# Gate-row buffers of the Fourier group moved into the room of the projection weights, and the loads of the last two stages put in another order on one queue

## The chip, the core and the metric

One core of a Trainium2 chip runs one program. The metric is the device time of one execution in microseconds (us), the median of several runs. The core's engines are TensorE (PE, with its weight load PEld), VectorE (DVE), ScalarE (ACT) and GpSimd (POOL); SyncE (SP) issues every transfer of this kernel, in the order in which they stand in its program, so all transfers share one queue.

## What is computed

One layer of a mixer over 2048 latent tokens of width 1024, with a prefix of 256 context tokens. One projection of the normalised input feeds two groups of heads, and their outputs go through one output projection:

```python
hx = rmsnorm(x, norm_w) * (1 + scale) + shift
u, zf, zs, xbc, dt = split(hx @ w_in)          # 512, 512, 1536, 2560, 48 columns
mixed = fft2(u, axes=(positions, 64 channels)).real @ w_fourier + b_fourier
four  = mixed * silu(zf)                       # Fourier group: 512 columns
xbc = silu(conv3x3(xbc) + conv_b)              # depthwise, then a scan over chunks of 128
y   = scan_forward(xbc, dt) + scan_backward(xbc, dt) + d_skip * xs
ssd = rmsnorm_by_group(y * silu(zs)) * ssd_norm_w
out = rmsnorm(x + gate * (concat(four, ssd) @ w_out)) * final_norm_w
```

## The kernel before, in words

All of it is fp32. A matrix product is done as three fp32r products of high and low parts (`hh`, `hl` hold the two parts of the normalised input for all tokens, 64 KB of each partition apiece; `wh`, `wl` those of one 128-column tile of projection weights). What each engine does next is fixed when the program is built: a scheduler lays out the instructions that the code issues, within their dependencies, and each engine then works through its own list in order.

The end of the kernel has three stages that matter here.

**Backward scan.** It runs beside projections of the gate columns `zs`, for token blocks 0 to 2. A weight tile is loaded by `weights` (L164 to L171) into `raw` (one buffer), split by ACT into `wh` and by POOL into `wl` (two buffers each), and used by 24 matmuls for each token block (L176 to L178). These buffers are in pool `wp` (stack `p1w`).

**Fourier stage** (from L863). Twelve weight tiles are loaded again for token block 3, `zs_ops([(i, (3,)) ...])`. `interleave` puts the Fourier work between their matmuls: `f_table` (from the loaded `w_fourier` and the 64-point tables), `f_step2` (the second step of the transform, from `g_d` and `tw`), and `f_mm(dt, h, i)`: 16 calls of 12 matmuls for four column tiles `dt` and two halves `h`. `f_gate` follows each pair: it adds the bias, and multiplies with the gate rows `zf` of that `dt`, a tile of 128 x 2048 (1 MB) that `zf_load` brings from `zfT_d`; pool `fb` has two such buffers. After its second half, `fm_d<-zf` stores the gated tile. What `interleave` has not placed is returned as `left` and issued afterwards.

**Unit stage** (`s1` to `s6`): 64 units (16 chunks by 4 groups). `s1` builds the decay matrix of a unit (small loads `rt`, `lt`, then `cb`, `chl`), `s2` and `s3` carry the state, `s4` and `s5` form and normalise the output, and `s6` multiplies with the output weights. These weights (16 MB as high and low parts) are loaded by `w_group(0)` to `w_group(3)`, eight loads of 512 KB each, into the rooms of `hh` and `hl` as these come free: group 0 after the last projection, group 1 after the `h = 0` half of the last `f_mm`, groups 2 and 3 after the `h = 1` half. `s6` of unit u needs group u mod 4, and for the Fourier columns a piece of `fm_d` (`fm_half`): columns 0 and 1 for groups 0 and 1, columns 2 and 3 for groups 2 and 3. `tc.issue_after(x)` keeps what is issued under it behind x on its queue.

As built, each transfer on SP's queue also waits until the transfer eight places ahead of it has landed, so at most eight are under way.

Of the kernel before, what the change touches and what calls it, by code (L numbers as in the profile page):

```python
# [9 lines left out]
F32 = mybir.dt.float32  # L10
# [8 lines left out]
P = 128  # L19
# [30 lines left out]
def mixer_layer(ctx: ExitStack, tc: tile.TileContext, A: dict, out: bass.AP, taps=None):  # L50
# [3 lines left out]
    def pool(name, bufs=1, space=None, stack=ctx, side=None):  # L54
        kw = {"space": space} if space is not None else {}
        if side is not None:
            kw["side"] = side
        if space != DRAM:
            kw["reuse_waits"] = "tile"
        return stack.enter_context(tc.tile_pool(name=name, bufs=bufs, **kw))  # L60
# [6 lines left out]
    def copy(dst, src):  # L67
        return nc.scalar.activation(dst, src, AF.Copy).ins  # L68
# [29 lines left out]
    def const_tile(name, where=const):  # L98
        a = A[name]
        t = where.tile(list(a.shape), F32, name="c_" + name)  # L100
        load(t, a)
        return t
# [37 lines left out]
    p1 = ctx.enter_context(ExitStack())  # L140
# [5 lines left out]
    p1w = ctx.enter_context(ExitStack())  # L146
# [609 lines left out]
    def interleave(main, side, lead, speed, finish=False):  # L756
        tm, ts = (sum(c for c, _ in o) for o in (main, side))
        am = as_ = 0.0
        n = 0
        for c, fn in main:  # L760
            fn()
            am += c
            while n < len(side) and am >= lead and as_ <= speed * ts * (am - lead) / tm:
                side[n][1]()
                as_ += side[n][0]
                n += 1
        for _, fn in side[n:] if finish else ():
            fn()
        return side[n:]

    with ExitStack() as psc:
        sp = pool("sp3", 2, stack=psc)
        st = {}
# [85 lines left out]
    def w_group(g):  # L859
        for n in range(4 * g, 4 * g + 4):  # L860
            w_load(n)

    pfb = ctx.enter_context(ExitStack())  # L863
    pfa = ctx.enter_context(ExitStack())
    fa = pool("fa", 2, stack=pfa)
    fb = pool("fb", 2, stack=pfb, side="right")
    c64 = [const_tile("c64", where=fa), const_tile("s64", where=fa)]
    tw64 = const_tile("tw64", where=fa)
    bf = const_tile("bf", where=fb)
    xe = fb.tile([P, 2, 2, 4, 16], F32R, name="xe", bufs=1)  # L870
    ye = fb.tile([P, 4, 16], F32, name="ye", bufs=1)
    fo = {"new": main_psum}
    gls = {}
    tws = {}
    zft = {}
# [19 lines left out]

    def zf_load(dt):
        def go():
            zf = zft[dt] = fb.tile([P, 16, P], F32, name="zf", tag="zf")
            load(zf[:].rearrange("p a b -> p (a b)"), zfT_d[dt])
            if dt != 2:  # L900
                nc.scalar.activation(zf, zf, AF.Silu)
            nc.gpsimd.tensor_tensor(out=zf[:, :, 64], in0=zf[:, :, 64], in1=ye[:, dt], op=ALU.mult)
        return go
# [41 lines left out]
    def f_gate(dt, p0, p1, parts):  # L945
        zf = zft[dt]
        q32 = fb.tile([P, 512], F32, name="q32", tag="q32", bufs=1)
        copy(q32, p1)
        for sign in range(2):
            yy = fb.tile([P, 512], F32, name="yy", tag="yy")  # L950
            nc.vector.scalar_tensor_tensor(out=yy, in0=p0, scalar=bf[:, dt:dt + 1], in1=q32,
                                           op0=ALU.add, op1=ALU.add if sign == 0 else ALU.subtract)
            for yv, k1, nt in parts[sign](yy):
                a = k1 if sign == 0 else P - k1 - nt * yv.shape[-1] + 1
                zv = zf[:, :, a:a + nt * yv.shape[-1]]
                if sign == 1:
                    zv = rev(zv)
                if nt > 1:
                    zv = zv.rearrange("p a (t b) -> p t a b", t=nt)
                (nc.vector if sign else nc.gpsimd).tensor_tensor(out=zv, in0=yv, in1=zv, op=ALU.mult)  # L960
# [44 lines left out]
    tw_load(0)  # L1005
    g_load(0, 0)
    P2 = {}
    dts = [0, 3, 1, 2]
    side = [(1.7, f_table(j)) for j in range(4)]
    for b in range(4):  # L1010
        side += [(0.9, f_step2(b, ct)) for ct in range(4)]
# [2 lines left out]
        if b == 1:  # L1014
            side += [(0.0, zf_load(dt)) for dt in dts[:2]]
    side.append((0.0, f_switch))
    fmm = [(dt, h) for dt in dts[:2] for h in range(2)] + [(dt, h) for h in range(2) for dt in dts[2:]]
    for n, (dt, h) in enumerate(fmm):
        if n in (4, 5):
            side.append((0.0, zf_load(dt)))  # L1020
        if n == 6:
            side.append((0.0, lambda: w_group(1)))
        side += [(2.6, f_mm(dt, h, i)) for i in range(2)]
    left = interleave(zs_ops([(i, (3,)) for i in range(19, 7, -1)]), side, 10, .75)
    wa1 = P2["wa1"]
    ones = const_tile("ones", wa1)
    msk = wa1.tile([P, P], U8, name="msk8", bufs=1)
# [11 lines left out]
    for t in lt:  # L1039
        nc.vector.tensor_copy(out=t, in_=st2[:, :2])  # L1040

    w_group(0)
    for _, fn in left:
        fn()
    p1.close()
    ps = pool("ps2", space=PSUM)
    fo["new"] = lambda: ps.tile([P, 512], F32, name="pft", tag="out", bufs=2)
# [39 lines left out]
    for u in range(2):  # L1087
        s1(u)
    pfb.close()
    p1w.close()  # L1090
    wk = pool("wk", 2)
    fnw = const_tile("fnw", wk)
    wa = pool("wa", 2)
# [151 lines left out]

    NU = NCH * G
    s2(0)
    for u in range(NU + 2):
        if u + 1 < NU:
            if u > 0:  # L1250
                s1(u + 1)
            s2(u + 1)
        if u < 2:
            with tc.issue_after(fo["st"]), tc.issue_after(units[u + 1]["ld"]):
                w_group(u + 2)
        if u < NU:
            s3(u)
            s4(u)
        if 1 <= u <= NU:
            s5(u - 1)  # L1260
        if u >= 2:
            s6(u - 2)
# [110 lines left out]
```

## Time and profile before

| | |
|---|---|
| time, median of 3 runs | 1911.37 us (1909.71 to 1916.48) |
| the profiled execution: its own time | 1912.61 us |
| its span, first to last instruction | 1910.8 us |
| PE busy | 1809.4 us, 95% of the span |
| DVE, ACT, POOL busy | 1258.5, 873.9, 906.2 us |
| mean granted TensorE clock | 0.977 |
| moved by SP's queue | 300 MB, 50.6% of the DMA engines' time |

The median of the runs stands 1.2 us below the profiled execution, and 1.8 us of that execution lie around its span. Busy times of PE are modelled ends of pipelined matmuls, so what PE waits for, and when it starts again, says more than its busy share.

### The profile page before, as it was taken

To read this page: it belongs to the slowest core of one execution; us is meant where nothing else is said; L and a number is where in the kernel's file an instruction comes from. 1 tells how busy PE (TensorE), PEld (TensorE's weight loads), DVE (VectorE), ACT (ScalarE), POOL (GpSimd) and SP (SyncE) were. 2 spreads that over 40 slices of the span, in tenths; PEclk is the share of its full clock that TensorE was granted. 3 is DMA by queue.
4 is the path that set the end of the run, shared out by engine and by line. 5 is a ranking of instruction groups with operands and counts; after the bars stand their busy time and mean duration, and the time that the engine had idled before them with its cause. 6 is when DMAs were issued, how large, how long until landed. Compare 5 with 4: busy or idle time off the path is not lost.

```text
span 1910.8 us, 28132 instructions
## 1 busy us (share of the span) xinstructions
PE 1809.4 (95%) x9142; PEld 1492.4 (78%) x9142; DVE 1258.5 (66%) x1809; ACT 873.9 (46%) x1968; POOL 906.2 (47%) x791
## 2 busy tenths in 40 slices
PE   6989999999999999989999999957999999999997
PEld 2779988888888888878888877845778777777776
DVE  3744569788888897557665622334677777667865
ACT  3632235445445455346666653223444444435443
POOL 1320034224123134178787732145777777668742
PEclk8999999999999999999999999977999999999999
DMA  7432344535445345367776774786445444444441
GB/s 256 166 93 77 90 131 151 171 113 166 138 130 160 122 129 174 120 200 217 213 218 206 216 247 136 224 287 218 125 143 151 130 132 134 147 124 138 144 137 44
DMA packets 291332, 301.80 MB, mean 158 GB/s; under 512 B 34098, under 2 KB 242066, under 8 KB 290675
## 3 DMA queue, kind: packets, MB, share of 16 engines
q1 hardware_dynamic: 291186, 300.01, 50.6%
q8 instruction: 73, 1.20, 0.3%
q14 instruction: 73, 0.59, 0.1%
HBM read 196.82 MB, written 103.10 MB: 157 GB/s over the span
## 4 chain that ended last, share of the span: by engine, by line
PE 75%; DMA 9%; DVE 5%; POOL 5%; issue 3%; ACT 2%; SPq 1%; POOLq 0%; DVEq 0%; ACTq 0%
PE pj L178 11%; PE pj L177 11%; PE pj L176 11%; PE po L1212 6%; PE po L1210 6%; PE po L1211 6%; PE py L1151 2%; PE parg L1079 2%; POOL sl L72 2%; PE pj L508 1%; PE pj L509 1%; PE pj L510 1%; PE py L1154 1%; DMA ev<-in_wout 1%; PE ptr L569 1%
## 5 line engine op out<-in xcount | busy, mean ns | idle before, releaser
L178 PE MATMUL pj<-hh,wl 128*128 128x512 f32 x1152 | 452.6, 393 | 0.8 <-POOL wl L72 0.8
L177 PE MATMUL pj<-hl,wh 128*128 128x512 f32 x1152 | 452.1, 392 | 0.0
L176 PE MATMUL pj<-hh,wh 128*128 128x512 f32 x1152 | 450.0, 394 | 2.1 <-ACT img L68 1.6
L636 DVE SCALAR_TENSOR_TENSOR pacc<-img,c_convw,pacc 128x1024 f32<-128x1024 f32 x320 | 410.0, 1287 | 58.5 <-ACT pacc L633 49.2
L72 POOL TENSOR_TENSOR wl<-raw,wh 128x1024 fp32r<-128x1024 f32 x48 | 116.5, 2428 | 345.4 <-ACT wh L68 294.8
L178 PEld LDWEIGHTS pj<-hh,wl 128*128 128x128 f32 x1152 | 216.4, 188 | 47.4 <-POOL wl L72 1.4
L176 PEld LDWEIGHTS pj<-hh,wh 128*128 128x128 f32 x1152 | 217.0, 188 | 44.4 <-ACT img L68 2.3
L177 PEld LDWEIGHTS pj<-hl,wh 128*128 128x128 f32 x1152 | 216.6, 188 | 40.9 <-issue 1.8
L807 ACT ACTIVATE xd<-xt,smb 128x64 f32<-128x64 f32 x384 | 100.8, 336 | 80.2 <-POOL yb L811 78.5
L1210 PE MATMUL po<-hl,mh 128*128 128x512 f32 x288 | 117.5, 408 | 0.7 <-ACT mh L68 0.4
L1211 PE MATMUL po<-hh,mh 128*128 128x512 f32 x288 | 114.8, 399 | 0.0
L1081 DVE COPY_PREDICATED parg<-msk,parg 128x384 f32<-128x384 uint8 x128 | 71.1, 556 | 64.1 <-PE parg L1079 63.7
L1212 PE MATMUL po<-hl,ml 128*128 128x512 f32 x288 | 109.8, 401 | 2.6 <-POOL ml L72 2.4
L1083 ACT ACTIVATE w<-parg 128x384 f32<-128x384 f32 x128 | 62.3, 486 | 104.8 <-DVE parg L1081 104.5
L72 DVE TENSOR_TENSOR xl<-xw,xh 128x384 fp32r<-128x384 f32 x76 | 63.7, 843 | 59.3 <-ACT xh L68 57.9
L1120 POOL TENSOR_TENSOR ts<-ts,yb 128x384 f32<-128x384 f32 x64 | 73.6, 1150 | 57.6 <-issue 27.2
L1079 PE MATMUL parg<-rt,lt 128*128 128x384 f32 x256 | 88.0, 372 | 11.2 <-DMA rt<-cum_d 4.1
L72 POOL TENSOR_TENSOR ml<-gt,mh 128x384 fp32r<-128x384 f32 x64 | 68.4, 1068 | 58.8 <-ACT mh L68 55.4
L68 ACT ACTIVATE xh<-xw 128x384 fp32r<-128x384 f32 x136 | 69.9, 516 | 55.2 <-PE pst L1138 14.9
L1084 DVE TENSOR_TENSOR w<-w,cb 128x768 f32<-128x768 f32 x64 | 81.6, 1275 | 12.1 <-ACT w L1083 10.9
L72 DVE TENSOR_TENSOR sl<-hbk,sh 128x384 fp32r<-128x384 f32 x64 | 59.9, 937 | 38.4 <-ACT sh L68 38.2
L72 POOL TENSOR_TENSOR sl<-ev,sh 128x512 fp32r<-128x512 f32 x32 | 42.1, 1317 | 89.1 <-DMA wo_d<-sl 38.3
(388 smaller groups left out, 4132.7 us busy)
## 6 DMA issues: line engine op xcount, KB each, us to landing
raw<-in_win SPq DMA_DIRECT2D x48, 512.0 KB
xt<-xtok_d SPq DMA_DIRECT2D x80, 192.0 KB
xtok_d<-tk SPq DMA_DIRECT2D x48, 256.0 KB
zsT_d<-ev SPq DMA_DIRECT2D x48, 256.0 KB
yb_d<-yb SPq DMA_DIRECT2D x64, 192.0 KB
yb<-yb_d SPq DMA_DIRECT2D x64, 192.0 KB
zs<-zsT_d SPq DMA_DIRECT2D x64, 192.0 KB
xg<-xtok_d SPq DMA_DIRECT2D x64, 192.0 KB
```

The costliest lines, as they stand in the source:

```text
L72: (lo_engine or nc.vector).tensor_tensor(out=lo, in0=src, in1=hi.bitcast(F32), op=ALU.subtract)
L176: mm(po, wh[:, k], a, start=(k == 0), stop=False)
L177: mm(po, wh[:, k], b, start=False, stop=False)
L178: done["mm"] = mm(po, wl[:, k], a, start=False, stop=(k == KT - 1)).ins
L636: nc.vector.scalar_tensor_tensor(out=acc, in0=im[:, r0 + dy:r0 + dy + 16, dx:dx + GRID_W], scalar=tap(t), in1=acc, op0=ALU.mult, op1=ALU.add)
L807: nc.scalar.activation(xd[:, h], d["x"][:, h], AF.Copy, scale=smb[:, 3, c, g * HG + h:g * HG + h + 1])
L1079: mm(po, l[:, dr], r[:, cols], start=True, stop=True)
L1084: nc.vector.tensor_tensor(out=w, in0=w, in1=cb[:].unsqueeze(1).broadcast_to([P, HG, P]), op=ALU.mult)
L1120: nc.gpsimd.tensor_tensor(out=ts, in0=ts, in1=yb, op=ALU.add)
L1210: mm(po, a, wh[:, i], start=(g == 0 and q == 0), stop=False)
L1211: mm(po, a, wl[:, i], start=False, stop=False)
L1212: mm(po, b, wh[:, i], start=False, stop=(g == 3 and q == 3))
```

## The change

The pool of projection weights `wp` is closed at the start of the Fourier stage, and a new one of the same kind, `wp2`, opened behind the pool `fb`. `wp2` in turn is closed after the last projection, and a pool `fz` with two buffers for gate rows takes its room. The order of the column tiles becomes 0, 1, 3, 2. All work of the first two is interleaved with the projections; the other two, with their gate rows loaded into `fz`, follow. Weight group 1 is issued between their halves, as before; group 2 is issued right after `s2(0)`, group 3 after `s2(1)`, and neither is kept behind the last store of gated rows.

```diff
--- before.py
+++ after.py
@@ -863,13 +863,17 @@
     pfb = ctx.enter_context(ExitStack())
     pfa = ctx.enter_context(ExitStack())
     fa = pool("fa", 2, stack=pfa)
+    p1w.close()
     fb = pool("fb", 2, stack=pfb, side="right")
+    p2w = ctx.enter_context(ExitStack())
+    W["p"] = pool("wp2", 2, stack=p2w, side="right")
     c64 = [const_tile("c64", where=fa), const_tile("s64", where=fa)]
     tw64 = const_tile("tw64", where=fa)
     bf = const_tile("bf", where=fb)
     xe = fb.tile([P, 2, 2, 4, 16], F32R, name="xe", bufs=1)
     ye = fb.tile([P, 4, 16], F32, name="ye", bufs=1)
     fo = {"new": main_psum}
+    fz = {"p": fb}
     gls = {}
     tws = {}
     zft = {}
@@ -895,7 +899,7 @@
 
     def zf_load(dt):
         def go():
-            zf = zft[dt] = fb.tile([P, 16, P], F32, name="zf", tag="zf")
+            zf = zft[dt] = fz["p"].tile([P, 16, P], F32, name="zf", tag="zf")
             load(zf[:].rearrange("p a b -> p (a b)"), zfT_d[dt])
             if dt != 2:
                 nc.scalar.activation(zf, zf, AF.Silu)
@@ -945,7 +949,7 @@
     def f_gate(dt, p0, p1, parts):
         zf = zft[dt]
         q32 = fb.tile([P, 512], F32, name="q32", tag="q32", bufs=1)
-        copy(q32, p1)
+        fo["q"] = copy(q32, p1)
         for sign in range(2):
             yy = fb.tile([P, 512], F32, name="yy", tag="yy")
             nc.vector.scalar_tensor_tensor(out=yy, in0=p0, scalar=bf[:, dt:dt + 1], in1=q32,
@@ -1005,7 +1009,7 @@
     tw_load(0)
     g_load(0, 0)
     P2 = {}
-    dts = [0, 3, 1, 2]
+    dts = [0, 1, 3, 2]
     side = [(1.7, f_table(j)) for j in range(4)]
     for b in range(4):
         side += [(0.9, f_step2(b, ct)) for ct in range(4)]
@@ -1014,14 +1018,11 @@
         if b == 1:
             side += [(0.0, zf_load(dt)) for dt in dts[:2]]
     side.append((0.0, f_switch))
-    fmm = [(dt, h) for dt in dts[:2] for h in range(2)] + [(dt, h) for h in range(2) for dt in dts[2:]]
-    for n, (dt, h) in enumerate(fmm):
-        if n in (4, 5):
-            side.append((0.0, zf_load(dt)))
-        if n == 6:
-            side.append((0.0, lambda: w_group(1)))
-        side += [(2.6, f_mm(dt, h, i)) for i in range(2)]
-    left = interleave(zs_ops([(i, (3,)) for i in range(19, 7, -1)]), side, 10, .75)
+    for dt in dts[:2]:
+        side += [(2.6, f_mm(dt, h, i)) for h in range(2) for i in range(2)]
+    interleave(zs_ops([(i, (3,)) for i in range(19, 7, -1)]), side, 10, 1, True)
+    p2w.close()
+    fz["p"] = pool("fz", 2, stack=pfb, side="right")
     wa1 = P2["wa1"]
     ones = const_tile("ones", wa1)
     msk = wa1.tile([P, P], U8, name="msk8", bufs=1)
@@ -1039,9 +1040,15 @@
     for t in lt:
         nc.vector.tensor_copy(out=t, in_=st2[:, :2])
 
+    for dt in dts[2:]:
+        zf_load(dt)()
     w_group(0)
-    for _, fn in left:
-        fn()
+    for h in range(2):
+        for dt in dts[2:]:
+            for i in range(2):
+                f_mm(dt, h, i)()
+        if h == 0:
+            w_group(1)
     p1.close()
     ps = pool("ps2", space=PSUM)
     fo["new"] = lambda: ps.tile([P, 512], F32, name="pft", tag="out", bufs=2)
@@ -1087,7 +1094,6 @@
     for u in range(2):
         s1(u)
     pfb.close()
-    p1w.close()
     wk = pool("wk", 2)
     fnw = const_tile("fnw", wk)
     wa = pool("wa", 2)
@@ -1245,14 +1251,16 @@
 
     NU = NCH * G
     s2(0)
+    with tc.issue_after(units[0]["ld"]):
+        w_group(2)
     for u in range(NU + 2):
         if u + 1 < NU:
             if u > 0:
                 s1(u + 1)
             s2(u + 1)
-        if u < 2:
-            with tc.issue_after(fo["st"]), tc.issue_after(units[u + 1]["ld"]):
-                w_group(u + 2)
+            if u == 0:
+                with tc.issue_after(units[1]["ld"]):
+                    w_group(3)
         if u < NU:
             s3(u)
             s4(u)
```

SP's queue around the start of the Fourier stage, before (`raw` is a tile of projection weights, `yb_d<-yb` a store of the scan, `c_c`, `c_s`, `c_tw` the tables c64, s64, tw64, `gl<-in_wf` the four pieces of `w_fourier`, two of the twelve `raw` stand further up):

```order
L63 DMA raw<-in_win 128x1024
L63 DMA yb_d<-yb_10425 128x384
L63 DMA zsT_d<-ev 128x4x128
L63 DMA c_c_10453<-in_c 128x128
L63 DMA c_s_10455<-in_s 128x128
L63 DMA c_tw_10457<-in_tw 128x32
L63 DMA c_bf<-in_bf 128x4
L63 DMA gl<-in_wf 128x512 x4
L63 DMA tw<-in_tw 128x512
L63 DMA gl<-g_d 128x512
L63 DMA zsT_d<-ev 128x4x128
L63 DMA gl<-g_d 128x512
```

and after the change:

```order
L63 DMA yb_d<-yb_10425 128x384
L63 DMA c_bf<-in_bf 128x4
L63 DMA zf<-zfT_d 128x2048 x2
L63 DMA c_c_10457<-in_c 128x128
L63 DMA c_s_10459<-in_s 128x128
L63 DMA c_tw_10461<-in_tw 128x32
L63 DMA gl<-in_wf 128x512 x4
L63 DMA tw<-in_tw 128x512
L63 DMA gl<-g_d 128x512
L63 DMA raw<-in_win 128x1024
```

Before, the `raw` shown is the second of block 3, and the gate rows of the first two column tiles follow as `zf<-zfT_d` four rows further down. Now these stand ahead of the tables and of `w_fourier`, and the first weight tile of block 3 is the last row shown, behind them all.

PE at the same place, before. Between the scan's last L802 and the first table (L909) stand 48 projection matmuls of token block 3, two weight tiles. The last of them and the table:

```order
L176 MATMUL pj<-hh,wh 128x512
L177 MATMUL pj<-hl,wh 128x512
L178 MATMUL pj<-hh,wl 128x512
L909 MATMUL pj<-gl,c_c_10453 128x512
L909 MATMUL pj<-gl,c_s_10455 128x512
L176 MATMUL pj<-hh,wh 128x512
```

and after, from the scan's last matmul (L927 and L935 are `f_step2`, L909 and L923 before):

```order
L804 MATMUL pj<-sh_10417,cc_10365 128x384
L927 MATMUL ptr<-tw,gl 128x128 x4
L935 MATMUL ptr<-c_tw_10461,gl 128x32
L176 MATMUL pj<-hh,wh 128x512
L177 MATMUL pj<-hl,wh 128x512
L927 MATMUL ptr<-tw,gl 128x128 x4
L935 MATMUL ptr<-c_tw_10461,gl 128x32
L178 MATMUL pj<-hh,wl 128x512
```

No projection of token block 3 stands ahead of the first Fourier work any more; the first L176 uses the `raw` at the end of SP's rows above.

SP's queue at the end of the Fourier stage, before (`hl<-wo_d` and `hh<-wo_d` are weight groups, the `rt`, `lt`, `cb`, `chl` behind them unit 2's loads):

```order
L63 DMA fm_d<-zf 128x16x128
L63 DMA hl<-wo_d 128x2x512 x8
L63 DMA zf<-zfT_d 128x2048
L63 DMA fm_d<-zf 128x16x128 x2
L63 DMA hl<-wo_d 128x2x512
L63 DMA hh<-wo_d 128x2x512
L63 DMA hl<-wo_d 128x2x512
L63 DMA hh<-wo_d 128x2x512
L63 DMA hl<-wo_d 128x2x512
L63 DMA hh<-wo_d 128x2x512
L63 DMA hl<-wo_d 128x2x512
L63 DMA hh<-wo_d 128x2x512
```

and after:

```order
L63 DMA fm_d<-zf 128x16x128
L63 DMA zf<-zfT_d 128x2048 x2
L63 DMA hl<-wo_d 128x2x512 x8
L63 DMA hh<-wo_d 128x2x512
L63 DMA hl<-wo_d 128x2x512
L63 DMA hh<-wo_d 128x2x512 x2
L63 DMA hl<-wo_d 128x2x512
L63 DMA hh<-wo_d 128x2x512
L63 DMA hl<-wo_d 128x2x512
L63 DMA hh<-wo_d 128x2x512
L63 DMA fm_d<-zf 128x16x128
L63 DMA hl<-wo_d 128x2x512
```

Both late gate rows moved ahead of weight group 1. Behind the rows shown, the change has `hh<-wo_d` five times, the last store `fm_d<-zf`, `hh<-wo_d` twice, and only then unit 2's `lt` and `rt`, while before these stand between groups 2 and 3.

## Rows read from the trace of the kernel before

**Rows 1.** The page: its span, and the granted clock in 40 slices.

```profile
span 1910.8 us, 28132 instructions
...
PEclk8999999999999999999999999977999999999999
```

**Rows 2.** Windows: stretch, its length, busy time by engine (instructions), clock, DMA share, GB/s.

```profile
1120.00:1215.00 95.00, 93.39 (x461) 72.97 (x461) 24.54 (x52) 36.89 (x69) 23.23 (x13) 1.00 0.53 179
1215.00:1250.00 35.00, 35.00 (x156) 29.00 (x155) 11.74 (x16) 8.91 (x13) 11.88 (x12) 1.00 0.97 308
1250.00:1268.00 18.00, 1.53 (x7) 1.17 (x6) 5.37 (x8) 0.60 (x1) 4.38 (x4) 0.60 0.65 242
...
1316.00:1335.00 19.00, 18.01 (x103) 14.67 (x102) 10.25 (x20) 6.92 (x16) 14.20 (x15) 1.00 0.66 191
```

**Rows 3.** Waits of PE, 1250 to 1316 us: total us, times, longest.

```profile
PE pyo L1115 <- DVE yy L951: 16.5, 1, 16.5
PE pyo L1115 <- DMA chl<-chl_d: 3.6, 3, 1.9
```

**Rows 4.** PE in time: start us, us, what [idle before it, its releaser].

```profile
1109.26 0.34 PE L802 MATMUL pj<-sh,cc 128*128 128x384 f32 x1
...
1121.54 1.10 PE L909 MATMUL pj<-gl,c_c 128*128 128x512 f32 x2 [0.65 <-DMA gl<-in_wf]
```

**Rows 5.** PE in time at the end of the Fourier stage and after.

```profile
1250.34 0.51 PE L1079 MATMUL parg<-rt,lt 128*128 128x384 f32 x2
1267.32 0.66 PE L1115 MATMUL pyo<-sh,chl 128*128 128x384 f32 x1 [16.47 <-DVE yy L951]
...
1289.52 0.66 PE L1079 MATMUL parg<-rt,lt 128*128 128x384 f32 x2 [2.08 <-DMA lt<-q_d]
...
1308.69 0.69 PE L1115 MATMUL pyo<-sh,chl 128*128 128x384 f32 x1 [1.85 <-DMA chl<-chl_d]
...
1312.70 0.42 PE L1115 MATMUL pyo<-sh,chl 128*128 128x384 f32 x1 [1.08 <-DMA chl<-chl_d]
```

**Rows 6.** SP in time: start of issue us, us, transfer.

```profile
1118.60 1.86 SPq L63 DMA_DIRECT2D gl<-in_wf  x4
...
1122.62 0.82 SPq L63 DMA_DIRECT2D raw<-in_win  x1
...
1240.97 8.29 SPq L63 DMA_DIRECT2D hl<-wo_d  x8
1249.31 1.23 SPq L63 DMA_DIRECT2D zf<-zfT_d  x1
...
1278.05 0.26 SPq L63 DMA_DIRECT2D rt<-cum_d  x1
...
1289.98 5.64 SPq L63 DMA_DIRECT2D hh<-wo_d  x8
```

**Rows 7.** POOL in time around the end of the scan.

```profile
1110.37 2.40 POOL L72 TENSOR_TENSOR wl<-raw,wh 128x1024 fp32r<-128x1024 f32 x1 [0.29 <-ACT wh L68]
1112.73 1.00 POOL L811 TENSOR_TENSOR yb<-yb,xd 128x384 f32<-128x384 f32 x1
```

**Rows 8.** ACT in time: the first weight tile split in the Fourier stage.

```profile
1130.09 1.06 ACT L68 ACTIVATE wh<-raw 128x1024 fp32r<-128x1024 f32 x1 [1.43 <-DMA raw<-in_win]
```

**Rows 9.** Windows of 4 us in the Fourier stage, columns as in rows 2.

```profile
1124.00:1128.00 4.00, 4.00 (x17) 2.95 (x16) 0.69 (x1) 0.13 (x1) 0.00 (x0) 1.00 0.99 291
1128.00:1132.00 4.00, 4.00 (x14) 2.32 (x13) 1.03 (x2) 2.51 (x4) 0.78 (x1) 1.00 1.05 430
```

**Rows 10.** The chain that ended last: start us, us, piece.

```profile
1132.43 0.89 PE ptr L923 x8
...
1142.86 5.14 DMA raw<-in_win
...
1249.31 12.74 DMA zf<-zfT_d
...
1318.58 2.65 DMA fr<-fm_d
```

## Prediction, made before the changed kernel was run

> **What bounds the kernel now.** I read the page first: PE's granted clock falls in two slices out of forty, near 1290 us of 1910.8 [rows 1]. The windows by stage place it. From 1120 to 1250 us PE hardly rests (93.4 of 95 us, 35.0 of 35 us); from 1250 to 1268 it works 1.5 of 18 us at a clock of 0.60, that is, part of the time at 1.2 instead of 2.4 GHz; from 1316 on it is full again [rows 2]. So the kernel is bound by PE except where the Fourier stage hands over to the unit stage. The waits say for what: once 16.5 us for DVE's gate, then 3.6 us for transfers of unit data [rows 3]. In time: the last `f_mm` ends at 1250.34, PE starts again at 1267.32, waits for unit 2's rows until 1289.52, for unit 3's and 4's data until 1308.69 and 1312.70, and from there on it runs [rows 5]. The hand-over thus takes 62.4 us. The cause of the first wait is on SP's queue: the last gate rows were issued behind eight weight loads (8.29 us of issue, no matmul needed them yet) and took 12.74 us [rows 6, 10].
>
> At the other end of the stage nothing is lost today: between the scan's end and the first table PE waits 0.65 us [rows 4].
>
> **The change, part by part.** T is the end of the last `f_mm`, 1250.34 before.
>
> *Start of the Fourier stage: a loss.* Before, 48 matmuls of two weight tiles loaded during the scan (11 us) hid the loads of `w_fourier`, the tables and the first rows of `g_d`. Now PE's work ends with the scan, at about 1110.0 (L802 starts at 1109.26, two more of its kind follow at once [rows 4]). What is late next is the first weight tile, since it may only be issued behind the queue shown above. Step by step:
> - The last store of the scan needs POOL's `yb`. That stood behind a split of 2.40 us that falls away [rows 7], so the store goes out near 1112 instead of 1113.8, and the two gate-row loads at 1112.5 and 1113.
> - Rate: 12.74 us for 1 MB behind seven loads of 512 KB, 4.7 MB, is 370 GB/s; a load of 128 KB takes 2.65 us, so some 2.3 us come on top [rows 10]. The second gate-row load lands at 1112.5 + 2.3 + 2.1 MB / 370 = 1120.5.
> - `tw` stands eight places behind it and waits for it; `tw`, `gl` and `raw` are issued by 1121.5. Between it and the weights lie 2.24 MB (tables 0.15, `w_fourier` 1.05, `tw` and `gl` 0.52, `raw` 0.52). Stretches of this stage moved 291 to 430 GB/s [rows 9]: 5.2 to 7.7 us, landing 1125.7 to 1128.2. I take 1127; before, the `raw` issued at 1122.62 was split at 1130.09 [rows 6, 8], 7.5 us, about the same.
> - ACT's split takes 1.06 us [rows 8]: first projection at 1128.2. PE stands from 1110.0 to there, 18.2 us. One `f_step2` (0.89 us and a small matmul, 1.1) moves into the gap [rows 10], and the old wait of 0.65 goes: 16.4 us. The third matmul needs POOL's 2.40 us [rows 7]; the second `f_step2` covers 1.1 of that: +0.9.
> - After such a stand PE restarts at half clock: at 1308.69 a 384-column matmul shows 0.69 us, at 1312.70 again 0.42 [rows 5]. Four us at half speed lose 2.0.
> - Later tiles come one every 5.14 + 1.06 + 2.40 = 8.6 us (load, ACT, POOL) [rows 7, 8, 10]; PE spends 108 us on twelve of them with what is interleaved, 9.0 each, so this hides on average; 1.0 for tiles with less beside them, at most 5.5 if the cycle is 9.1 throughout.
>
> Sum: 16.4 + 0.9 + 2.0 + 1.0 = 20.3 us later at T. Low end 14 (weights at 1124.6, as if nothing lay in front of them, and no loss of clock), high end 26 (1128.2 and the 5.5).
>
> *Gate rows earlier: a gain that is not all kept.* After dt 1's last matmul come 96 others (8 halves of 12, 0.228 us each, 21.9 us). Its gate takes up to 5.3 us (before, from the rows' landing at 1262.05 to PE's start at 1267.32 with one and a half gates [rows 5, 10]), so the second store and both gate rows are issued near T - 17.5. 3.1 MB at 370 GB/s and the rest of weight group 0 put them at T - 8. The last gate then ends 4 to 5 us after T instead of 17: units 0 and 1 start 12 us sooner. Those units' own chain then lasts as before, some 14 us, to T + 19.
>
> *All weight groups ahead of unit 2: where the gain is held up.* From T - 8 the queue carries group 1 (4.2 MB), groups 2 and 3 (8.4 MB) and two stores (2.1 MB): 14.7 MB at 370 GB/s, 39.7 us, to T + 32. Unit 2's `lt` and `rt` were issued before group 3 until now, at 1278.05 [rows 6], and PE took them up at T + 39.2 [rows 5]. Now they land near T + 32.5. PE waits from T + 19 to there, a new wait of 13 us. POOL, DVE and ACT wait with it, since the state of unit 2 hangs on the same loads, and `fm_half` for unit 0 stands behind them too, although its rows were stored long ago.
>
> *From there to full speed.* Before, 23.2 us (1289.52 to 1312.70). 4.2 MB of group 3 (issued from 1289.98 [rows 6]), 11.3 us, lay in them and do so no longer; but the 18 matmuls of `s6(0)` that ran in PE's gaps before now follow here, 18 x 0.23 = 4.1. T + 32.5 + 11.9 + 4.1 = T + 48.5 against T + 62.4: 13.9 us regained. I take 13, as two units' small loads (some 30 at 0.4 us of issue) now come in one row. Bounds: 8, if these are taken one after the other behind each landing, and 21, if the last two terms shrink to 9.
>
> The other edits cost nothing: the same matmuls, splits and bytes; the copy result that `f_gate` now keeps is not used on the chip. DVE and POOL have room for the gates: 24.5 and 23.2 of 95 us in the Fourier stage, 10.3 and 14.2 of 19 behind it [rows 2].
>
> **Sum.** +20.3 - 13 = +7.3 us. The profiled execution took 1912.6 us (1.8 around its span), so it would take 1919.9; the median of the runs is 1.2 below it, which makes 1918.5. Bounds: +14 - 21 = -7 (1904) and +26 - 8 = +18 (1929).
>
> The rate of 370 GB/s carries both terms. The Trainium skill, "DMA: Bandwidth & Descriptors", section "Specifications", gives some 358 GB/s as HBM's limit for a core. With that rate the gate rows and weights would come 0.4 us later and the weight groups 1.3 us later: 1920. The trace does not bear it out as a limit: a stretch of 4 us moved 430 GB/s [rows 9].
>
> **Rivals.** A change smaller than 0.5%, 9.6 us, can't be told from none here.
> - *Slower, over 9.6 us* (likeliest 1924): the same loss of 20, but little regained, because PE gains nothing from a gate that ends sooner when unit 2's rows wait behind the last weights. For: the rows that end the second wait are transfers [rows 3, 5]. Against: no group lies between units 2 and 3 any more. It decides where less than 10.7 us comes back, that is, full speed later than T + 51.7.
> - *Faster, over 9.6 us* (likeliest 1900): the hand-over shrinks to what PE has to do. If unit 2's and 3's data land together at T + 32.5 and PE runs at full clock from T + 35, 27 us come back, against a loss of 16 at the lower end. For: nothing big stands behind the weights any more. Against: before, 23.2 us passed from unit 2's rows to full speed, of which group 3 explains 11.3 [rows 5, 6]. It decides where more than 30 comes back at a loss of 20.
> - *The change doesn't do what it says*: the late gate rows stand behind the second store, which waits for a gate; if that is late by 12 us, they land after T as before. PE would then wait 16 us for the gate again, but that wait would end near T + 16 and units 0 and 1 at T + 31, still ahead of unit 2's rows. It costs some 3 us: 1921.
>
> **How the numbers follow.** My forecast, 1918.5 with 1910 to 1921 as its own range, has 0.49; the slower rival 0.37, the faster one 0.08, the idle change 0.06 (half of it past the bound). So faster 0.08, same 0.52, slower 0.40. The range for 8 in 10 leaves out the faster rival and the far end of the slower one: 1904 to 1929, the bounds of the sum.
>
> **What would show it.** Right: PE stands some 17 to 18 us from 1110, ended by a weight split or `raw`; the clock is low there; `f_mm` ends near 1270; PE waits under 6 us for the gate, then some 13 us for `lt`, `rt` or `chl`, and runs freely by T + 49. Wrong: the first projection of block 3 before 1122, which would take half of the loss away; a wait for the gate over 10 us; or PE busy through T + 19 to T + 32.

## The result, and the profile after

The changed kernel takes 1916.0 us (median of 20 runs, 1912.5 to 1921.4) against 1911.2 for the kernel before (20 runs): a ratio of 1.0025 with a 95% interval of 1.0016 to 1.0033. It is slower by 4.85 us, which is within the 0.5% that was set as "no change"; 1918.5 had been forecast. One slow execution (of the run a_nog3, 2032 us at a mean granted clock of 0.84) is left out of all numbers below. The page of the profiled execution shows a second place where the granted clock falls, the slice from 1100 to 1148 us, ahead of those of the hand-over:

```profile
span 1913.1 us, 28131 instructions
...
PEclk8999999999999999999999979987999999999999
```

Three stretches of both kernels, as windows (columns as in [rows 2]): from the end of the scan's last matmul to T (the start of the first `parg` matmul, which follows the last `f_mm` at once), from T to 1361 us, and from there to the end. First before, then after:

```profile
1111.33:1250.34 139.01, 137.40 (x654) 109.38 (x654) 36.84 (x69) 47.46 (x83) 39.84 (x27) 1.00 0.65 212
1250.34:1361.00 110.66, 72.58 (x354) 56.31 (x352) 56.17 (x99) 34.56 (x83) 60.61 (x59) 0.77 0.69 224
1361.00:1910.83 549.83, 525.41 (x2903) 420.43 (x2900) 390.83 (x722) 241.62 (x617) 363.78 (x343) 0.99 0.42 128
```

```profile
1108.13:1266.78 158.65, 141.07 (x660) 113.61 (x661) 35.89 (x72) 48.33 (x83) 38.69 (x23) 0.94 0.63 203
1266.78:1361.00 94.22, 61.61 (x311) 48.00 (x310) 46.20 (x82) 30.58 (x73) 54.34 (x54) 0.80 0.70 226
1361.00:1913.05 552.05, 529.64 (x2944) 424.61 (x2942) 403.81 (x738) 246.14 (x630) 376.72 (x353) 0.99 0.44 131
```

The Fourier stage is 19.6 us longer (158.65 against 139.01), all that follows is 14.2 us shorter (646.3 against 660.5): together +5.4, which is the 4.85 of the medians within what single executions differ. The scan before it ended 3.2 us earlier in this execution; PE's progress was already 1.8 us ahead in the middle of the scan, which the change doesn't touch; the other 1.4 us are six projection matmuls of token block 3 that stood among the scan's last ones before and stand behind them now. So the stages are compared by their lengths. Idle time of PE is length less busy time.

Of the 14.2 us, 7.5 are idle time behind T (55.0 against 62.5) and 6.7 busy time, of the same matmuls (591.3 against 598.0). The busy time is the clock. Over the stretches behind T in which 1.2 GHz were granted (0.50 in the rows), the windows sum up to this, before and after:

```profile
sum 60.02, PE 28.28 PEld 21.94 DVE 27.31 ACT 15.78 POOL 20.86; mean PE 4.71 PEld 3.66 DVE 4.55 ACT 2.63 POOL 3.48
```

```profile
sum 43.85, PE 14.68 PEld 12.13 DVE 11.47 ACT 8.83 POOL 14.81; mean PE 3.67 PEld 3.03 DVE 2.87 ACT 2.21 POOL 3.70
```

PE worked 28.3 us at half clock before and 14.7 after. At full clock that work would have taken half as long, 14.1 and 7.3 us less, a difference of 6.8 us, which is all of the 6.7. Time at half clock in which PE stands costs nothing: after the change one such stretch, 27.3 us from 1282.11, has only 5.8 us of work in it.

*The start of the Fourier stage.* PE, SP and ACT in time (start, length, what, in brackets the idle time before it and what ended it), then a window of the stretch in which PE starts again:

```profile
1125.61 2.05 PE L927 MATMUL ptr<-tw,gl 128*128 128x128 f32 x8 [17.48 <-DMA gl<-g_d]
1128.02 0.79 PE L176 MATMUL pj<-hh,wh 128*128 128x512 f32 x1
1131.03 0.77 PE L178 MATMUL pj<-hh,wl 128*128 128x512 f32 x1
```

```profile
1110.82 0.88 SPq L63 DMA_DIRECT2D zf<-zfT_d  x2
...
1119.02 0.33 SPq L63 DMA_DIRECT2D tw<-in_tw  x1
1119.39 0.43 SPq L63 DMA_DIRECT2D gl<-g_d  x1
1119.92 0.38 SPq L63 DMA_DIRECT2D raw<-in_win  x1
```

```profile
1119.08 1.91 ACT L905 ACTIVATE zf<-zf 128x2048 f32<-128x2048 f32 x1 [0.69 <-DMA zf<-zfT_d]
1126.91 1.06 ACT L68 ACTIVATE wh<-raw 128x1024 fp32r<-128x1024 f32 x1 [5.92 <-DMA raw<-in_win]
```

```profile
1125.61:1131.93 6.32, 6.22 (x24) 5.66 (x25) 1.47 (x5) 2.34 (x7) 2.36 (x1) 0.50 0.35 108
```

Before, PE waited 0.65 us here [rows 4]. Now it stands 17.48 us. The two gate rows go out first, `tw` stands until the second has landed (its `silu` starts at 1119.08, `tw` is issued at 1119.02), `raw` is split at 1126.91. It is the only wait of PE from the scan to T. For the first 6.3 us behind it the clock is 0.50.

*The hand-over.* PE and SP in time:

```profile
1272.03 0.69 PE L1086 MATMUL parg<-rt,lt 128*128 128x384 f32 x1 [4.74 <-DVE parg L1088]
...
1303.79 1.02 PE L1086 MATMUL parg<-rt,lt 128*128 128x384 f32 x2 [19.61 <-DMA rt<-cum_d]
...
1318.15 0.69 PE L1121 MATMUL pyo<-sh,chl 128*128 128x384 f32 x1 [0.81 <-DMA chl<-chl_d]
```

```profile
1250.64 0.37 SPq L63 DMA_DIRECT2D fm_d<-zf  x1
1251.30 4.03 SPq L63 DMA_DIRECT2D zf<-zfT_d  x2
...
1290.05 7.90 SPq L63 DMA_DIRECT2D hh<-wo_d  x2
1298.05 0.65 SPq L63 DMA_DIRECT2D lt<-q_d  x2
```

The wait for the gate is 4.74 us instead of 16.47 [rows 5]. Then PE stands 19.61 us for unit 2's `rt`, which is issued behind the last load of weight group 3. Windows of the transfers in this stretch, the second from T - 8 to the issue of unit 2's rows:

```profile
1255.00:1283.00 28.00, 19.69 (x98) 15.27 (x97) 15.32 (x23) 10.07 (x16) 17.91 (x18) 0.92 1.05 386
```

```profile
1258.78:1298.05 39.27, 17.09 (x86) 12.99 (x84) 15.88 (x24) 10.75 (x19) 21.02 (x21) 0.75 1.04 371
```

### The profile page after: what moved, and what is told of

The parts are those of the page before. It is cut to its first block, busy times and chain, and to the rows that moved or that the text cites. A ratio compares the mean times of both kernels' runs of the same rounds, so it can differ in the third digit from the quotient of the medians.

```text
span 1913.1 us, 28131 instructions
## 1 busy us (share of the span) xinstructions
PE 1805.5 (94%) x9142; PEld 1493.4 (78%) x9142; DVE 1261.7 (66%) x1809; ACT 874.3 (46%) x1968; POOL 907.0 (47%) x791
## 5 line engine op out<-in xcount | busy, mean ns | idle before, releaser
L176 PE MATMUL pj<-hh,wh 128*128 128x512 f32 x1152 | 450.7, 395 | 1.6 <-ACT img L68 1.5
L176 PEld LDWEIGHTS pj<-hh,wh 128*128 128x128 f32 x1152 | 217.7, 189 | 43.3 <-ACT img L68 1.7
L1086 PE MATMUL parg<-rt,lt 128*128 128x384 f32 x256 | 89.4, 372 | 28.8 <-DMA rt<-cum_d 19.6
L72 POOL TENSOR_TENSOR sl<-hf,sh 128x384 fp32r<-128x384 f32 x64 | 72.0, 1127 | 44.5 <-ACT sh L68 38.8
L1126 POOL TENSOR_TENSOR ts<-ts,yb 128x384 f32<-128x384 f32 x64 | 75.0, 1171 | 33.0 <-issue 17.5
L72 POOL TENSOR_TENSOR sl<-ev,sh 128x512 fp32r<-128x512 f32 x32 | 42.1, 1316 | 89.3 <-DMA wo_d<-sl 38.3
```

What stands on the lines that cost most here:

```text
L72: (lo_engine or nc.vector).tensor_tensor(out=lo, in0=src, in1=hi.bitcast(F32), op=ALU.subtract)
L176: mm(po, wh[:, k], a, start=(k == 0), stop=False)
L1086: mm(po, l[:, dr], r[:, cols], start=True, stop=True)
L1126: nc.gpsimd.tensor_tensor(out=ts, in0=ts, in1=yb, op=ALU.add)
```

## The experiments

Both kernels and twelve others, with the ratio to the kernel before (95% interval). That kernel was timed again beside each group of runs (medians 1909.4 to 1911.2 us), so the ratios compare better than the medians do; all are within 1%. The five columns behind it are worked out from windows like those above of each kernel's one profiled execution: length of the Fourier stage, PE's idle time from T to 1361 us and from there to the end, PE's busy time at half clock behind T, and the length from T to the end, in us.

| kernel | median us | ratio | Fourier | idle to 1361 | idle later | at half clock | T to end |
|---|---|---|---|---|---|---|---|
| before | 1911.2 | | 139.0 | 38.1 | 24.4 | 28.3 | 660.5 |
| changed | 1916.0 | 1.0025 (1.0016 to 1.0033) | 158.7 | 32.6 | 22.4 | 14.7 | 646.3 |
| start_only | 1917.5 | 1.0036 (1.0023 to 1.0049) | 158.7 | 31.6 | 21.3 | 21.3 | 646.1 |
| end_zf | 1919.9 | 1.0048 (1.0031 to 1.0064) | 138.3 | 43.7 | 25.5 | 39.2 | 670.1 |
| zf_late | 1913.2 | 1.0011 (1.0001 to 1.0021) | 155.8 | 30.0 | 22.3 | 18.1 | 644.5 |
| raw_first | 1925.2 | 1.0083 (1.0066 to 1.0100) | 152.1 | 40.8 | 27.5 | 22.1 | 661.2 |
| g3_late | 1922.3 | 1.0061 (1.0048 to 1.0073) | 158.4 | 30.3 | 24.3 | 23.9 | 651.0 |
| a_g23 | 1924.4 | 1.0076 (1.0060 to 1.0092) | 158.0 | 28.2 | 28.9 | 30.4 | 654.1 |
| a_nog3 | 1907.2 | 0.9984 (0.9970 to 0.9997) | 157.8 | 25.4 | 22.0 | 19.0 | 638.2 |
| b_zf | 1909.4 | 0.9998 (0.9988 to 1.0007) | 139.0 | 30.7 | 27.7 | 31.5 | 659.0 |
| b_g3 | 1907.2 | 0.9984 (0.9973 to 0.9996) | 139.0 | 30.0 | 24.1 | 34.0 | 655.7 |
| b_zf_g3 | 1908.5 | 0.9990 (0.9980 to 0.9999) | 138.8 | 29.0 | 27.4 | 36.4 | 658.9 |
| b_zf_g23 | 1908.8 | 0.9994 (0.9984 to 1.0004) | 138.9 | 27.9 | 28.6 | 35.6 | 657.2 |
| b_zf_pe | 1907.2 | 0.9983 (0.9971 to 0.9994) | 141.7 | 37.5 | 21.7 | 27.1 | 654.7 |

The length from T to the end, less the idle time and less half of the time at half clock, is 581.3 to 584.8 us in all fourteen. So what they differ by there, 32 us, is idle time and clock, but for 3.5 us at most.

**start_only**: the new start with the old end.

```diff
+    p1w.close()
     fb = pool("fb", 2, stack=pfb, side="right")
+    p2w = ctx.enter_context(ExitStack())
+    W["p"] = pool("wp2", 2, stack=p2w, side="right")
...
+    p2w.close()
     pfb.close()
-    p1w.close()
```

> Only the start of the change is done (the projection weights' pool is closed at the scan's end and opened again above fb); the order of dts, the gate-row buffers and the placing of the weight groups stay as before. Theory (two effects that add up: some 18 us lost at the scan's end, some 14 regained at the hand-over): PE stands 17 to 18 us after the scan as in the changed kernel, the last f_mm ends some 18 us later than before, PE then waits 16 us for the gate again, and the time is 1929 us (1925 to 1933). Rival (the loss at the start is small in the end, since unit data that come earlier absorb it, and the new tail regains little): the time is that of the changed kernel, 1916 us (1913 to 1920).

The time came out as the rival had it, not as the theory. The loss at the start is there in full (158.7), and PE waits 15.9 us for the gate again; yet T to the end takes 646.1 us, as in the changed kernel.

```profile
1282.92 1.21 PE L1082 MATMUL parg<-rt,lt 128*128 128x384 f32 x2 [15.86 <-DVE parg L1084]
```

SP's rows show one difference to before, whose share in this was not measured by itself: four of the six loads of unit 3's rows now stand ahead of group 3, which no line of the edit asked for; before, group 3 went out at 1289.98 [rows 6] and all six behind it, from 1296.18 on.

```profile
1301.37 0.24 SPq L63 DMA_DIRECT2D rt<-cum_d  x1
1301.70 0.34 SPq L63 DMA_DIRECT2D chl<-chl_d  x1
1302.27 0.82 SPq L63 DMA_DIRECT2D lt<-q_d  x2
1303.13 0.25 SPq L63 DMA_DIRECT2D rt<-cum_d  x1
1303.48 0.34 SPq L63 DMA_DIRECT2D bt<-bhl_d  x1
1303.87 2.83 SPq L63 DMA_DIRECT2D hh<-wo_d  x5
```

So the scheduler writes another order for the queues when an early stage moves, and what the changed kernel regains can be had without its new end.

**end_zf**: the new end on the old start (the order of `dts`, the loop of the last `f_mm` and the places of the four groups as in the change; the rows' buffers stay in `fb`).

```diff
-    dts = [0, 3, 1, 2]
+    dts = [0, 1, 3, 2]
...
+        if h == 0:
+            with tc.issue_after(zl[dts[3]]):
+                w_group(1)
```

> Only the end of the change, on the start of before: the projection weights' pool stays open, the order of dts, the last f_mm behind the projections and the placing of the four weight groups are those of the changed kernel. The two late gate rows come from fb (so the fourth waits for the second store) and stand ahead of weight group 1, as in the changed kernel. Theory (the two parts of the change add up): no stand at the scan's end, the gate is waited for 5 us instead of 16.5, unit 2's rows 13 to 20 us; 18 us less than the changed kernel, 1898 us (1894 to 1902). Rival (what the changed kernel regains comes with any hand-over that is late, as the kernel with only the new start showed, and the new end adds nothing): 1911 us (1907 to 1915).

Neither: it is the slower of the two halves. PE's waits from 1245 to 1361 us (total, times, longest):

```profile
PE parg L1082 <- DMA rt<-cum_d: 6.3, 1, 6.3
PE pyo L1118 <- DVE yy L952: 6.2, 1, 6.2
PE pn L1170 <- DVE s L1164: 6.2, 1, 6.2
PE po L1213 <- ACT fm L68: 6.1, 1, 6.1
PE pyo L1118 <- ACT q L68: 5.1, 1, 5.1
```

The long wait is gone and five of 5 to 6 us stand in its place. PE works 39.2 us at half clock, the most of all. By the ratios the new start costs 0.36% alone, the new end 0.48% alone, both together 0.25%: the two parts don't add up.

**zf_late** and **raw_first**: what the start's loss is made of. In zf_late the two early gate-row loads go behind the second weight tile; in raw_first the first tile also goes ahead of the tables (the last added line is in raw_first alone).

```diff
-            side += [(0.0, zf_load(dt)) for dt in dts[:2]]
+            side += [(0.0, zf_after(dt)) for dt in dts[:2]]
...
+            with tc.issue_after(done["raw"][n_raw + 1]):
+                zf_load(dt)()
...
+    zw["next"] = weights(19)
     c64 = [const_tile("c64", where=fa), const_tile("s64", where=fa)]
```

> The changed kernel with one move: the two early gate-row loads (1 MB each) are issued behind the second weight tile instead of ahead of the tables. Theory (PE's stand after the scan is the queue: tw stood behind the landing of the second gate-row load at 1119.0): tw, gl and raw are issued some 4 us earlier, the first projection starts near 1121.5 instead of 1128.0 us, and the time falls by 6 us to 1910 (1907 to 1912). Rival (tables and w_fourier alone take as long, or the second tile is late instead): the stand ends after 1126 and the time stays 1916 (1914 to 1918).

> The changed kernel with the first weight tile loaded ahead of the tables, and the gate rows behind the second tile. Theory (the queue decides): raw is issued near 1111 us, the first projection starts near 1116, its third matmul near 1118, the tables fill in behind; 8 us less than the changed kernel, 1908 (1904 to 1911). Rival (the second tile, which needs the one raw buffer and so waits for POOL's split, becomes the bound): the stand is only split in two, the sum of PE's waits from 1108 to 1135 stays over 14 us, and the time is 1914 (1912 to 1917).

zf_late: PE's first row, and SP's.

```profile
1126.45 2.05 PE L933 MATMUL ptr<-tw,gl 128*128 128x128 f32 x8 [13.86 <-DMA gl<-g_d]
```

```profile
1118.58 0.43 SPq L63 DMA_DIRECT2D tw<-in_tw  x1
1119.05 0.43 SPq L63 DMA_DIRECT2D gl<-g_d  x1
1119.58 0.38 SPq L63 DMA_DIRECT2D raw<-in_win  x1
```

The scan ended at 1112.60 here, so `raw` is issued 7.0 us behind it instead of 11.8. PE stands 13.9 instead of 17.5 us: the queue explains 3.6 us, about half of what was expected, and the stage is 2.8 us shorter. The median falls by as much, 2.85, to between theory and rival.

raw_first, PE's two waits at the start:

```profile
1118.18 0.80 PE L176 MATMUL pj<-hh,wh 128*128 128x512 f32 x1 [7.69 <-ACT wh L68]
1120.66 0.80 PE L178 MATMUL pj<-hh,wl 128*128 128x512 f32 x1 [1.26 <-POOL wl L72]
```

Here the start came out near the theory: the first projection starts 7.7 us behind the scan's end, the waits sum to 9.0 us where the rival had over 14, and the stage is 6.5 us shorter (8 expected). The kernel is still the slowest of all, which neither expected: PE waits 13.05 us for the gate instead of 4.74, as the second store and the gate rows behind it are issued 7.6 and 7.2 us before T instead of 16.1 and 15.5, and the later units idle 5 us more.

**g3_late**, **a_g23** and **a_nog3**: is the wait of 19.6 us the bytes ahead of unit 2's rows? The first issues group 3 behind unit 2's loads, the second also group 2 there and group 3 behind unit 3's, the third leaves the loads of group 3 out. The diff shows the lines of g3_late, then that of a_nog3 in `w_load`.

```diff
-            if u == 0:
-                with tc.issue_after(units[1]["ld"]):
+            if u == 1:
+                with tc.issue_after(units[2]["ld"]):
                     w_group(3)
...
-        for i in range(2):
+        for i in range(2 if n < 12 else 0):
```

> The changed kernel with weight group 3 issued behind unit 2's loads instead of ahead of them. Theory (PE's wait of 19.6 us for unit 2's rt is a place in the queue): the wait falls by some 11 us to 8 (4.2 MB at 370 GB/s no longer ahead), part of it comes back at unit 3 whose loads now stand behind group 3: 1910 us (1906 to 1913). Rival (the whole of the transfers bounds the stage: the wait is passed on to unit 3 in full, and full speed comes 51 us after the last f_mm as before): 1916 us (1914 to 1918).

> The changed kernel with weight group 2 issued behind unit 2's loads and group 3 behind unit 3's. Theory (only the place in the queue counts): the wait for unit 2's rows falls from 19.6 to under 6 us, later rows wait a few us each, and 10 us less than the changed kernel are taken: 1906 us (1902 to 1910). Rival (the bytes must come in the same stretch anyway, each unit's rows stand behind a group again, as where group 3 alone was moved): the waits sum to 20 us and more, 1916 us or above.

> The changed kernel without the loads of weight group 3 (4.2 MB of w_out are left out, so the last quarter of each output product takes stale weights; all matmuls still run). Theory (the wait of 19.6 us for unit 2's rows is the bytes ahead of them in the queue): it falls by 11 us to 8 or 9, and the time falls by as much less what half clock takes back: 1906 us (1903 to 1909). Rival (something other than these bytes sets when the units run freely): the wait moves on to a later row and the time stays above 1912.

a_nog3, PE in time, and the wait of g3_late:

```profile
1291.81 1.02 PE L1086 MATMUL parg<-rt,lt 128*128 128x384 f32 x2 [13.04 <-DMA rt<-cum_d]
```

```profile
PE parg L1086 <- DMA rt<-cum_d: 13.4, 1, 13.4
```

In a_nog3, without 4.2 MB, the rows are taken up at T + 25.2 instead of T + 37.0, 11.8 us earlier, and the kernel is some 8 us faster (0.9984 against 1.0025), as the theory had it: the bytes ahead do set when the rows come. The wait itself is 13.0 us, not 8 or 9, since PE also reaches it sooner. g3_late brings unit 2's rows as early (T + 24.9), and is 6 to 7 us slower than the changed kernel, slower than its theory and its rival had it. a_g23 brings them at T + 14.7 with a wait of 2.1 us and is slower still; its rival, not its theory, came true. Its largest waits up to 1361 us:

```profile
PE parg L1086 <- DVE parg L1088: 8.1, 4, 5.1
PE parg L1086 <- DMA lt<-q_d: 6.1, 1, 6.1
PE py L1157 <- DVE w L1091: 5.0, 1, 5.0
```

By the table a_g23 idles 4.4 us less to 1361 us and 6.5 more behind it, and its busy time behind T is 597.0 against 591.3 us, with 30.4 instead of 14.7 us of work at half clock. A sign of the reason for the later idle time lies in the program: from the twelfth unit on (the 48th `parg` matmul) PE's rows in a_nog3 and zf_late are those of the changed kernel one by one, and these three idle 22.0 to 22.4 us there, though their hand-overs differ; g3_late's and a_g23's differ from them in more than 20 pieces each, though only loads of the first four units were moved, and idle 24.3 and 28.9.

**b_zf**, **b_g3**, **b_zf_g3**, **b_zf_g23**: the kernel before with one move or two. b_zf issues group 1 behind the fourth gate row, b_g3 group 3 behind unit 3's loads; b_zf_g3 has both; b_zf_g23 has the first, with group 2 behind unit 3's loads and group 3 behind unit 4's. The diff shows b_zf, then b_g3.

```diff
-            side.append((0.0, lambda: w_group(1)))
+            side.append((0.0, w_late))
...
+        with tc.issue_after(zl[dts[3]]):
+            w_group(1)
...
-        if u < 2:
+        if u in (0, 2):
             with tc.issue_after(fo["st"]), tc.issue_after(units[u + 1]["ld"]):
-                w_group(u + 2)
+                w_group(2 + u // 2)
```

> The kernel before with one move: weight group 1 is issued behind the fourth gate-row load instead of ahead of it. Theory (the gate of the last f_mm is late because its rows stand behind eight weight loads): PE's wait for the gate falls from 16.5 to some 6 us, and all that is issued behind the gate's stores (group 2, unit 2's rows) comes earlier with it: 9 us less than before, 1902 us (1899 to 1906). Rival (unit 2's rows are bound by the transfers ahead of them, so the gate's gain turns into a longer wait for them): 1911 us (1908 to 1913).

> The kernel before with one move: weight group 3 is issued behind unit 3's loads instead of ahead of them. Theory (4.2 MB ahead of unit 3's and 4's rows make the waits of 4.1, 1.9 and 1.1 us and hold the clock low from 1291 to 1311): these waits fall away, 6 us less than before, 1905 us (1902 to 1908). Rival (group 3 then delays unit 4's rows by as much): 1911 us (1908 to 1914).

> The kernel before with both moves: group 1 behind the fourth gate-row load, group 3 behind unit 3's loads. Theory (both waits are places in one queue, and the gains add up): 15 us less than before, 1896 us (1892 to 1900). Rival (they overlap, or the transfers' sum bounds the stage): 1903 us or more.

> The kernel before with the fourth gate-row load ahead of weight group 1, group 2 behind unit 3's loads and group 3 behind unit 4's. Theory (with the gate's wait at 5 us, what is left of the hand-over are rows behind weight groups): idle time and half clock between the last f_mm and 1361 us fall from 50 to some 36 us: 1898 us (1894 to 1903). Rival (the waits move one unit on and the later stretch gives back what the hand-over gains, as with the other two orders): 1907 us (1904 to 1911).

b_zf, PE's waits from 1245 to 1361 us:

```profile
PE parg L1085 <- DMA rt<-cum_d: 10.0, 2, 8.6
PE pyo L1121 <- DVE yy L957: 5.7, 1, 5.7
```

The gate's wait falls from 16.5 to 5.7 us as intended, 8.6 us of it come back at a later unit's `rt`, and the later units idle 3.3 us more: no change, as the rival had it. The other three idle 8 to 10 us less in the hand-over, and are by their ratios 1 to 3 us faster than before where 6 to 15 were expected (for b_zf_g23 the interval takes in no change): b_g3 keeps the later idle time of before (24.1) and gains most, the other two give back 3 and 4 us there, and all three are busy 2.7 to 4.5 us longer behind T (600.7 to 602.5 against 598.0): by the table, half of their longer time at half clock is 2.9 to 4.1 us.

**b_zf_pe**: b_zf with two numbers of the call that mixes the Fourier stage's two streams.

```diff
-    left = interleave(zs_ops([(i, (3,)) for i in range(19, 7, -1)]), side, 10, .75)
+    left = interleave(zs_ops([(i, (3,)) for i in range(19, 7, -1)]), side, 11, 0.76)
```

> The kernel before with the fourth gate-row load ahead of weight group 1, as in the run of that name, and two numbers of the call that interleaves the Fourier stage changed (10 and 0.75 to 11 and 0.76). No load of the hand-over moves against that run, but the order written for PE from the twelfth unit on becomes that of the changed kernel, but for one row. Theory (the order of the later units costs more or less, and what a move in the hand-over gains is given back where it rewrites that order): idle time and half clock after 1361 us fall from 33 to some 22 us, and the time from 1909 to 1899 us (1896 to 1903). Rival (the later loss follows from when the units' data come, not from the order): 1909 us (1906 to 1912).

b_zf, then b_zf_pe, from 1361 us to the end:

```profile
1361.00:1909.68 548.68, 521.00 (x2853) 416.01 (x2851) 383.67 (x712) 238.21 (x608) 357.23 (x339) 0.99 0.41 126
```

```profile
1361.00:1905.44 544.44, 522.74 (x2897) 419.25 (x2895) 388.78 (x720) 241.01 (x617) 365.64 (x342) 0.99 0.43 130
```

Idle time there falls from 27.7 to 21.7 us with the written order of the later units, near what the changed kernel has: that half of the theory holds, with two reservations. The rows of DVE, ACT, POOL and SP are written in another order along with PE's, and the units come some 10 us later behind T here (the 48th `parg` matmul at T + 140.6 instead of T + 130.1). By the ratios the kernel is 0.15% faster than b_zf, 3 us and not 10: the Fourier stage is 2.7 us longer, and the order of the first units was rewritten too, so that PE waits for the gate 12.3 us again:

```profile
PE parg L1085 <- DVE parg L1087: 12.8, 2, 12.3
```

## Why the prediction was right, and where its reasons were not

*The start: mechanism and size right.* 20.3 us were forecast, the stage is 19.6 longer. The stand was ended by `gl<-g_d`, which is issued just ahead of `raw`, and not by `raw` or its split; the first projection follows at 1128.02, forecast 1128.2, though the scan had ended 1.9 us sooner than the forecast had it. PE's idle time rose by 16.0 (17.58 against 1.61), where 16.4 + 0.9 + 1.0 had been summed: the waits for POOL's split and for later tiles did not occur, as matmuls of `f_step2` covered the first split and no later tile was late. The term for the clock was too small: the stage's busy time rose by 3.7 us, of which 2.0 had been forecast for half clock. PE worked 6.2 us at half clock behind the stand, which is 3.1; the six matmuls more than before (660 against 654) are the smaller part. The gate rows ahead of `tw`, on which the step rested, are 3.6 us of the stand (zf_late); with tables and `w_fourier` out of the way of `raw` as well, 9.0 us are left of it (raw_first).

*The hand-over up to unit 2: right in kind, mis-sized.* The second store and the gate rows were issued at T - 16.1 and T - 15.5 (forecast T - 17.5), the gate's wait is 4.7 (under 6), units 0 and 1 run to T + 17.4 (19). The wait that takes the gate's place came, with 19.6 us instead of 13. "14.7 MB at 370 GB/s, to T + 32" held: from T - 8 to T + 31.3, when unit 2's first row was issued, the queue moved 371 GB/s, 14.6 MB. Mis-sized is the step behind it, "land near T + 32.5": 0.5 us were allowed from there to the rows, and PE took them up 5.7 us after the issue, at T + 37.0. PE ran on without long waits from T + 51.4 instead of T + 48.5, 11.0 us ahead of before instead of 13.9, and 0.3 us short of the point from which the slower rival decides. The waits for unit data before were also read too small: to the 3.6 us of `chl` [rows 3] come 4.1 for `rt` and 2.1 for `lt`.

The Trainium skill, "DMA: Bandwidth & Descriptors", section "Specifications", has some 358 GB/s as HBM's limit for a core. The trace does not agree: 39 us moved 371 GB/s here and 28 us 386, so the figure is no ceiling in this kernel.

*From full speed to the end: not in the prediction.* 3.2 us more came back there, which makes 14.2 where 13 had been summed: 5.3 us less idle time (22.4 against 27.7), and 2.0 more busy time, as 16 matmuls more were still to do. That the sum met the measurement is in part luck: this gain and the missing 3 us of the hand-over took each other away.

*The cause given for the regained time does not hold.* "Gate rows earlier: a gain" took the shorter wait for the gate as what is regained, and the sum has no term for the clock behind T, which gave back 6.7 of the 14.2 us. b_zf shortens that wait by 10.8 us on the kernel before and gains nothing; start_only keeps the wait and regains the same 14 us; end_zf has the short wait and loses 10. Shown is that the time behind T goes by PE's idle time and its work at half clock, and that the bytes ahead of unit data on SP's queue set part of it (a_nog3: 4.2 MB less are some 8 us less). That the order written for the later units sets their idle time is likely and not shown by itself: it goes with 6 us between b_zf and b_zf_pe, and three kernels with one order idle alike. Not settled is why kernels with the late start have the shorter rest as a group (638 to 654 us behind T, but 661 in raw_first; 655 to 670 with the old start). b_g3 and b_zf_pe are faster than both kernels, by 0.16% and 0.17% against before; no run has the hand-over of b_g3 and the later order of the changed kernel.

*The rivals.* "Slower, because unit 2's rows wait behind the last weights" was the nearest: its wait is the one that was measured. "The change doesn't do what it says" is out, since the rows were in time. "Faster" needed one landing for units 2 and 3 and full clock from T + 35; PE stood still until T + 37.

## What to carry to other kernels

Read a stall that is taken away together with what stands in the queue behind it: here 11 us less waiting for a gate were worth nothing, neither alone (b_zf) nor with group 3 moved as well (b_zf_g3 gains 1.9 us, b_g3 without the shorter wait 3.1). Where a scheduler writes the order, compare the written order far behind the edit before the trace is explained by the edit: kernels with the same rows for PE from the twelfth unit on idled the same 22.0 to 22.4 us there, the others 21.3 to 28.9. Account by stage with lengths, idle time and busy time of the same matmuls, and sum PE's work in the stretches at half clock, so that the clock is seen as a cost of its own.

## What was not expected of the hardware

Removing idle time did not remove time in step, since short waits cost clock as well. Behind T the same matmuls were busy 590.8 us (a_nog3) to 602.5 (b_zf_g3), with 19.0 and 36.4 us of work at half clock, which explains 8.7 of the 11.7 us. a_g23, with no wait over 6.1 us, idled 4.4 us less up to 1361 us than the changed kernel with its one wait of 19.6, and was busy 5.7 us longer in all: it worked 30.4 us at half clock against 14.7, while the long wait itself filled 19.6 of the 43.9 us that the changed kernel had at half clock behind T. And the transfers held 386 GB/s for 28 us on one core.
